# A decoder step on one Trainium2 core: the second MLP product in seven products of half size

## The chip, the cores and the metric

The kernel runs on one core of a Trainium2 chip. Its engines are TensorE (PE, matmuls; its weight loads are shown as PEld), VectorE (DVE), ScalarE (ACT), GpSimd (POOL) and SyncE (SP), whose queue issues most of the DMAs. Matmuls write to PSUM; everything else lies in SBUF or in DRAM. The metric is the device time of one execution in microseconds, the median of the runs shown.

## What is computed

One step of a decoder trunk with 1024 prompt tokens and 8 samples, all in fp32, T = 1032 columns in all. The change is in the last part, a gated MLP with a residual, followed by a norm:

```python
h = rmsnorm(x, g_ffn) * (1.0 + sc_f) + sh_f
a, b = jnp.split(h @ w_ffn_in, [D_FF], axis=-1)        # D_FF = 2816
...  # acc: causal convolution of width 3 over a
f = (jax.nn.silu(acc + conv_b) * b) @ w_ffn_out        # 2816 -> 1024
x = x + gt_f * f
...
yp = rmsnorm(yp, g_final); ys = rmsnorm(ys, g_final)
```

## The kernel before

Activations lie with channels on the 128 partitions and tokens in columns. A token half is HALF = 516 columns, a quarter QUART = 258; NS = 8 sample columns end the second half. An fp32 operand is split into two fp32r tiles, high and low: `split2` (L824) makes the high one with a cast on ScalarE and the low one with a subtraction on VectorE. A product is then three matmuls: high by high, high by low, low by high.

The first MLP product (L949 to L951 in `prod`, tiles pA and pS) already runs as seven products of half size (Winograd's form of Strassen's scheme). Its moving operands B11, B21, B22 and T1 to T4 are sums of quarters of h, made once; its weights A11, A12, A22 and S1 to S4 are quarters of a weight tile or sums of them, which GpSimd forms (L1099). The work goes f tile by f tile (FT = 22 tiles of 128 channels), seven steps of 24 matmuls each. `go` (L1254) does a step: it loads weights ten steps ahead, issues the products, splits one later weight (`prep`), and evacuates the result from PSUM (`evac`). After step A12 and S4 the convolution follows (L1149, L1154 and L1157), and `out_f` (L1159) multiplies the two branches on GpSimd and stores a half of an f tile to the DRAM tile `fd`, laid out by f.

The second product (L1402 to L1422) reads f and the weights back in groups of 2 to 4 f tiles (FFN_GROUPS). For each group it goes over 4 quarters and 8 output tiles m: `ffn_mm` does 3 matmuls per f tile, and `add_gated` (L1337) adds the result, times the gate, to a tile of xs, which `load_x` (L1316) loads from `x2d`. So each group adds to all of xs anew. In the last group the final norm follows quarter by quarter (`last_steps`, `final_a` to `final_last`).

PSUM serves both products through `banks` (L918), a ring of four tiles of two banks each. SBUF pools: `m0p` has four slots, which B11 and B21 hold until the last f tile; `gr` (12 slots) takes the place of the pools of the first product; `rw` has four buffers for what has just been loaded. `load2` and `split_f` load and split a tile; the first group's are put four steps before the end of the first product. The instructions of each engine are ordered by a scheduler, which goes by the order of the program and by when operands are ready.

## Time and profile before

| | |
|---|---|
| median of 3 runs | 1283.18 us (1282.71 to 1284.1) |
| profiled execution | 1283.75 us, its span 1282.0 us |
| TensorE busy | 1236.0 us in 9640 matmuls |
| VectorE, ScalarE, GpSimd busy | 821.0, 450.8, 389.8 us |
| mean granted clock of TensorE | 0.982 of full speed |

The span is the time from the first to the last instruction; the other 1.75 us of the profiled execution lie around it. A line such as L1379 is a line of the kernel. A row of a group gives the line, engine, operation, output and inputs, shapes and count, then busy time and the mean of one, and then the idle time of the engine just before it with what ended it.

### The profile page before, as it was taken

What the parts mean: (1) busy time and instruction counts of PE and PEld (TensorE: products, weight loads), DVE (VectorE), ACT (ScalarE), POOL (GpSimd) and SP (SyncE); (2) the same over time, 40 slices, a digit from 0 to 9 for tenths busy, and PEclk for the clock granted to TensorE, in tenths of its full rate; (3) what the DMA queues carried; (4) which work ended last, traced back from release to release, by engine and by line L of the source; (5) the groups of instructions that cost most, each with busy time, mean ns of one, the idle gap of its engine ahead of it and who ended that gap; (6) DMA issues with size and microseconds to landing.
All of it is one profiled execution on the core that took longest, in us unless ns stands there. A gap on an engine that the chain in (4) does not pass through costs nothing.

```text
span 1282.0 us, 24007 instructions
## 1 busy us (share of the span) xinstructions
PE 1236.0 (96%) x9640; PEld 1199.7 (94%) x9640; DVE 821.0 (64%) x1647; ACT 450.8 (35%) x878; POOL 389.8 (30%) x381
## 2 busy tenths in 40 slices
PE   8899999999999999968999999999999799999996
PEld 6799999999999999868999999999999799999996
DVE  4875556465753522789778777777777766676345
ACT  4453343342423411454334333343434301122053
POOL 3441111111330011464645545454553000000033
PEclk9999999999999999889999999999999899999998
DMA  8725444444410543102412222131224623332002
GB/s 319 273 59 178 122 137 156 125 140 152 143 44 1 207 151 106 39 28 74 145 64 99 75 76 78 71 100 63 88 75 141 238 83 100 100 128 71 1 34 100
DMA packets 78079, 140.57 MB, mean 110 GB/s; under 512 B 10928, under 2 KB 50064, under 8 KB 77968
## 3 DMA queue, kind: packets, MB, share of 16 engines
q1 hardware_dynamic: 74624, 138.09, 32.7%
q8 instruction: 76, 1.25, 0.4%
q10 hardware_dynamic: 3344, 0.95, 0.3%
q14 instruction: 35, 0.29, 0.1%
HBM read 115.00 MB, written 24.01 MB: 108 GB/s over the span
## 4 chain that ended last, share of the span: by engine, by line
PE 85%; DVE 7%; POOL 3%; DMA 2%; issue 1%; ACT 1%; DVEq 0%; SPq 0%; POOLq 0%; ACTq 0%
PE z L333 7%; PE z L334 7%; PE z L335 7%; PE fo L1379 6%; PE pS L949 6%; PE pS L951 6%; PE pS L950 6%; PE fo L1381 6%; PE fo L1380 6%; PE pA L950 5%; PE pA L949 5%; PE pA L951 5%; PE mo L949 2%; PE mo L951 2%; PE mo L950 2%; PE ada_ps L237 1%
## 5 line engine op out<-in xcount | busy, mean ns | idle before, releaser
L1379 PE MATMUL fo<-fhl,whl 128*128 128x258 f32 x704 | 198.0, 290 | 9.4 <-DVE xs L1344 9.1
L333 PE MATMUL z<-h_hi,hi_in 128*128 128x384 f32 (+1 forms) x624 | 203.7, 329 | 0.6 <-ACT h_hi L361 0.6
L334 PE MATMUL z<-h_lo,hi_in 128*128 128x384 f32 (+1 forms) x624 | 199.6, 320 | 0.2 <-DVE h_lo L362 0.2
L335 PE MATMUL z<-h_hi,lo_in 128*128 128x384 f32 (+1 forms) x624 | 198.7, 319 | 0.1
L1380 PE MATMUL fo<-fhl,whl 128*128 128x258 f32 x704 | 197.4, 283 | 0.0
L1381 PE MATMUL fo<-fhl,whl 128*128 128x258 f32 x704 | 195.4, 283 | 0.0
L949 PE MATMUL pS<-T,w_S 128*128 128x258 f32 x528 | 150.8, 286 | 6.5 <-ACT T L825 4.7
L950 PE MATMUL pS<-T,w_S 128*128 128x258 f32 x528 | 150.4, 285 | 5.0 <-DVE T L822 5.0
L951 PE MATMUL pS<-T,w_S 128*128 128x258 f32 x528 | 150.1, 284 | 0.0
L1344 DVE SCALAR_TENSOR_TENSOR xs<-fo,modT,xs 128x258 f32<-128x258 f32 (+1 forms) x224 | 104.5, 480 | 68.3 <-PE fo L1381 66.1
L1379 PEld LDWEIGHTS fo<-fhl,whl 128*128 128x128 f32 x704 | 132.3, 190 | 12.3 <-DVE xs L1344 10.3
L1380 PEld LDWEIGHTS fo<-fhl,whl 128*128 128x128 f32 x704 | 134.1, 190 | 0.0
L1381 PEld LDWEIGHTS fo<-fhl,whl 128*128 128x128 f32 x704 | 132.6, 190 | 0.0
L333 PEld LDWEIGHTS z<-h_hi,hi_in 128*128 128x128 f32 x624 | 117.2, 188 | 14.8 <-issue 12.8
L1161 POOL TENSOR_TENSOR mix_all<-mix_all 128x516 f32<-128x516 f32 x44 | 63.2, 1438 | 184.6 <-DVE mix_all L1115 159.6
L334 PEld LDWEIGHTS z<-h_lo,hi_in 128*128 128x128 f32 x624 | 117.9, 189 | 1.4 <-DVE h_lo L362 1.0
L335 PEld LDWEIGHTS z<-h_hi,lo_in 128*128 128x128 f32 x624 | 117.4, 188 | 0.5 <-DVE lo_in L215 0.4
L949 PEld LDWEIGHTS pS<-T,w_S 128*128 128x128 f32 x528 | 101.1, 191 | 7.3 <-ACT T L825 4.9
L950 PEld LDWEIGHTS pS<-T,w_S 128*128 128x128 f32 x528 | 101.0, 191 | 5.5 <-DVE T L822 5.5
L825 ACT CAST w_S<-S 128x512 fp32r<-128x512 f32 x88 | 54.5, 620 | 142.3 <-PE pS L951 87.9
L951 PEld LDWEIGHTS pS<-T,w_S 128*128 128x128 f32 x528 | 101.2, 192 | 0.0
L1154 DVE SCALAR_TENSOR_TENSOR mix_all<-mix_all,pa 128x508 f32<-128x508 f32 (+1 forms) x80 | 91.2, 1140 | 7.1 <-ACT mix_all L1149 4.9
(249 smaller groups left out, 3129.8 us busy)
## 6 DMA issues: line engine op xcount, KB each, us to landing
raw_ada<-w_ada SPq DMA_DIRECT2D x64, 256.0 KB, 3.5
raw_in<-w_in SPq DMA_DIRECT2D x26, 512.0 KB, 4.2
raw_a<-w_fin SPq DMA_DIRECT2D x25, 512.0 KB, 3.6
fd<-mix_all SPq DMA_DIRECT2D x44, 258.0 KB, 2.9
raw_fo<-fd SPq DMA_DIRECT2D x22, 516.0 KB, 4.5
raw_b<-w_fin SPq DMA_DIRECT2D x22, 512.0 KB, 3.6
raw_wo<-w_fout SPq DMA_DIRECT2D x22, 512.0 KB, 4.3
x2d<-mix_all SPq DMA_DIRECT2D x16, 258.0 KB, 2.4
```

Source lines behind the costliest of these rows:

```text
L333: mm(ps[:, 0:n], hi[:, ws], xh[:, k, 0:n], start=first, stop=False)
L334: mm(ps[:, 0:n], hi[:, ws], xl[:, k, 0:n], start=False, stop=False)
L335: mm(ps[:, 0:n], lo[:, ws], xh[:, k, 0:n], start=False, stop=last)
L949: mm(o, w[0][:, ks], b[:, 0, cols], start=first and kk == 0, stop=False)
L950: mm(o, w[0][:, ks], b[:, 1, cols], start=False, stop=False)
L951: mm(o, w[1][:, ks], b[:, 0, cols], start=False, stop=end)
L1154: nc.vector.scalar_tensor_tensor(s[:, 0:np_], a[:, i:i + np_], cw(i, f), s[:, 0:np_], ALU.mult, ALU.add)
L1161: nc.gpsimd.tensor_tensor(s, s, Bt.pop((f, t)), op=ALU.mult)
L1344: nc.vector.scalar_tensor_tensor(dst[:, 0:np_], ps[:, 0:np_], gt_f[:, m, 0:1], dst[:, 0:np_], ALU.mult, ALU.add)
L1379: mm(o, w[:, 0, ms_], v[:, 0, cols], start=i == 0, stop=False)
L1380: mm(o, w[:, 0, ms_], v[:, 1, cols], start=False, stop=False)
L1381: mm(o, w[:, 1, ms_], v[:, 0, cols], start=False, stop=i == len(fs) - 1)
```

## The change

The second product takes the same form as the first. Its output (1024 channels by 1032 columns) is cut in two by channels (4 m tiles each) and by columns (HALF each), and its inner dimension in two by f tiles: tile k with tile k + 11, for FH = 11 values of k. Seven products follow in the order of OUT_PRODS. In each, k is the outer loop, and four PSUM tiles collect all 4 m by 2 quarters; the last NLATE = 3 values of k run m by m, so that tiles end one after another.

The moving operands B11, B21, B22 and T1 to T4 of this product are made where f is made. The f tiles now come in pairs (FSEQ: 0, 11, 1, 12, ...). After an f tile `out_f` stores three of the four quarters, and the differences T1 to T4 are made on VectorE (`sum_t`), one per step of `go`, from the queue `late`; each is stored to `fd`, which now holds 7 x 11 tiles of half width. The weight sums S1 to S4 are made as the weights come in (`split_o`): S1 and S4 on GpSimd, S2 and S3 on VectorE. Operands come in 77 pairs (moving tile and weight), loaded and split NAHEAD = 8 pairs ahead (`ahead`). The first four go into m0p, and are split four steps before the end of the first product.

Results are kept as running sums in SBUF (Uo and W5) and added to xs, which is loaded from x2d in four parts of 4 m tiles by half. The final norm runs over halves and quarters in the last product. The diff, cut to its core:

```diff
+FH = FT // 2
+OUT_PRODS = (("A11", "B11"), ("A12", "B21"), ("S1", "T1"), ("S2", "T2"), ("S4", "B22"), ("S3", "T3"), ("A22", "T4"))
+FSEQ = tuple(f for k in range(FH) for f in (k, k + FH))
+
+NLATE = 3
+NAHEAD = 8
...
-    fd = dp.tile([FT, P, T], F32, tag="fd", name="fd")
+    fd = dp.tile([len(OUT_PRODS) * FH, P, HALF], F32, tag="fd", name="fd")
+    FD = {b: i * FH for i, (_, b) in enumerate(OUT_PRODS)}
...
     def out_f(f, t):
         s = Ft.pop((f, t))
         nc.gpsimd.tensor_tensor(s, s, Bt.pop((f, t)), op=ALU.mult)
-        nc.sync.dma_start(fd[f, :, t * HALF:(t + 1) * HALF], s)
+        k, i = f % FH, f // FH
+        Fo[k, i, t] = s
+        if (i, t) != (0, 1):
+            store_f(("B11", "B21", "B22")[i + t], k, s)
+        if (k, i, 1 - t) in Fo:
+            late.extend([lambda: sum_t(k, "T1", (0, 0), (0, 1), (0, 0))] if i == 0 else [
+                lambda: sum_t(k, "T3", (0, 1), (1, 1), (0, 1)), lambda: sum_t(k, "T2", (1, 1), (1, 1), (0, 0)),
+                lambda: sum_t(k, "T4", (1, 0), (1, 0), (1, 1))])
+
+    def store_f(name, k, s):
+        nc.sync.dma_start(fd[FD[name] + k], s)
+
+
+    Fo, late = {}, deque()
+
+    def sum_t(k, name, dst, a, b):
+        for i, t in {a, b}:
+            assert vown[vidx[f"f{k + FH * i}_{t}"]] == f"f{k + FH * i}_{t}"
+        nc.vector.tensor_tensor(Fo[k, dst[0], dst[1]], Fo[k, a[0], a[1]], Fo[k, b[0], b[1]], op=ALU.subtract)
+        store_f(name, k, Fo[k, dst[0], dst[1]])
...
-    HELD = (0, 1)
+    HELD = FSEQ[0:2]
     order = [(f, n) for n in ("S4", "S2", "S3", "S1", "A22") for f in HELD]
-    order += [(f, n) for f in range(2, NLEAD) for n in NAMES[2:]]
-    order += [(f, n) for f in range(NLEAD, FT) for n in NAMES]
+    order += [(f, n) for f in FSEQ[2:NLEAD] for n in NAMES[2:]]
+    order += [(f, n) for f in FSEQ[NLEAD:] for n in NAMES]
...
     def go(n, ev=True):
@@ -1259,12 +1288,14 @@
         prep()
         if ev:
             evac(f, name)
+        if late:
+            late.popleft()()
...
+    items = [(p, k) for p in range(len(OUT_PRODS)) for k in range(FH)]
+    WSRC = {"A11": (0, 0), "A12": (1, 0), "S1": (1, 1), "S2": (0, 0), "S4": (1, 0), "S3": (1, 1), "A22": (1, 1)}
...
+    def load_o(n=1):
+        for _ in range(min(n, len(to_load))):
+            p, k = to_load.popleft()
+            wn, bn = OUT_PRODS[p]
+            i, j = WSRC[wn]
+            v = oraw[p, k] = rw.tile([P, T], F32, tag="raw", name=f"raw_o{p}_{k}")
+            nc.sync.dma_start(v[:, 0:HALF], fd[FD[bn] + k])
+            if wn == "S1":
+                nc.sync.dma_start(sb[:, k], w_fout[k, :, 512:1024])
+            nc.sync.dma_start(v[:, HALF:HALF + 512], w_fout[k + FH * i, :, j * 512:(j + 1) * 512])
+
+    def split_o(n=1):
+        for _ in range(min(n, len(to_split))):
+            p, k = to_split.popleft()
+            wn = OUT_PRODS[p][0]
+            v = oraw.pop((p, k))
+            w = v[:, HALF:HALF + 512]
+            if wn == "S1":
+                nc.gpsimd.tensor_tensor(sb[:, k], sb[:, k], w, op=ALU.add)
+                w = sb[:, k]
+            elif wn == "S2":
+                nc.vector.tensor_tensor(sb[:, k], sb[:, k], w, op=ALU.subtract)
+                w = sb[:, k]
+            elif wn[0] == "S":
+                (nc.gpsimd if wn == "S4" else nc.vector).tensor_tensor(w, w, sb[:, k], op=ALU.subtract)
+            if k < 4:
+                u = m0p.tile([P, 2, 2, HALF], F32R, tag="m", name=f"o{p}_{k}")
+            else:
+                u = gr.tile([P, 2, 2, HALF], F32R, tag="g", name=f"o{p}_{k}")
+            ou[p, k] = u[:, 0], u[:, 1, :, 0:512]
+            split2(ou[p, k][0], v[:, 0:HALF])
+            split2(ou[p, k][1], w)
...
     for n in range(8, len(order)):
         go(n)
         if n == len(order) - 4:
+            load_o(4)
+            split_o(4)
+    while late:
+        late.popleft()()
...
+    gr = ctx.enter_context(tc.tile_pool(name="gr", bufs=8, side="right", reuse_waits="tile"))
+    uo = ctx.enter_context(tc.tile_pool(name="uo", bufs=1, side="right", reuse_waits="tile"))
+    f2 = ctx.enter_context(tc.tile_pool(name="f2", bufs=3, reuse_waits="tile"))
...
+    sb = uo.tile([P, FH, 512], F32, name="sb")
+    W5 = uo.tile([P, 4, HALF], F32, name="w5")
+    acc3 = [uo.tile([P, HALF], F32, name=f"acc3_{t}") for t in range(2)]
+    R3 = [uo.tile([P, HALF], F32, name=f"R3_{t}") for t in range(2)]
+    Uo = e1p.tile([P, 4, HALF], F32, tag="e", name="uo")
+    xs = vxp.tile([P, KT, 1036], F32, tag="v", name="xs")
...
+    def out_mm(o, p, k, m, s, first, last):
+        b, w = ou[p, k]
+        cols = slice(s * QUART, (s + 1) * QUART)
+        ms_ = slice(m * P, (m + 1) * P)
+        mm(o, w[:, 0, ms_], b[:, 0, cols], start=first, stop=False)
+        mm(o, w[:, 0, ms_], b[:, 1, cols], start=False, stop=False)
+        mm(o, w[:, 1, ms_], b[:, 0, cols], start=False, stop=last)
...
+    def before(name):
+        if name == "A12":
+            for m in range(4):
+                gated(m, 0, Uo[:, m])
+        elif name == "S4":
+            st12 = uo.tile([P, 4, NS], F32, name="st12")
+            nc.vector.tensor_tensor(st12, Uo[:, :, SC], W5[:, :, SC], op=ALU.add)
+            for m in range(4):
+                gated(m, 1, Uo[:, m, 0:HALF - NS])
+                gated(m, 1, W5[:, m, 0:HALF - NS])
+            return st12
+        elif name == "S3":
+            for m in range(4):
+                gated(m + 4, 1, W5[:, m, 0:HALF - NS])
+        elif name == "A22":
+            for m in range(4):
+                gated(m + 4, 0, Uo[:, m])
+
+    def after(name, m, ps, st):
+        v = ps[:, :, 0:QUART]
+        if name == "A11":
+            nc.scalar.copy(two(Uo[:, m]), v)
+        elif name == "A12":
+            gated(m, 0, v)
+            sq_sum(m, 0, m == 0, nc.gpsimd)
+        elif name == "S1":
+            nc.scalar.copy(two(W5[:, m]), v)
+        elif name == "S2":
+            nc.vector.tensor_tensor(two(Uo[:, m]), v, two(Uo[:, m]), op=ALU.add)
+        elif name == "S4":
+            gated(m, 1, v)
+            nc.vector.tensor_tensor(st[:, m], ps[:, 1, QUART - NS:QUART], st[:, m], op=ALU.add)
+            if m == 3:
+                gated_samples(0, st)
+                for i in range(4):
+                    sq_sum(i, 1, i == 0, nc.gpsimd)
+        elif name == "S3":
+            nc.vector.tensor_tensor(two(Uo[:, m]), v, two(Uo[:, m]), op=ALU.add)
+            gated(m + 4, 1, Uo[:, m, 0:HALF - NS])
...
+    def ahead(i):
+        load_o(max(0, i + NAHEAD + 3 - (len(items) - len(to_load))))
+        split_o(max(0, i + NAHEAD + 1 - (len(items) - len(to_split))))
+
+    XLOADS = {(0, 7): (0, 0), (2, 0): (0, 1), (3, 0): (4, 1), (4, 0): (4, 0)}
+    for p, (wn, bn) in enumerate(OUT_PRODS[:-1]):
+        ps = [banks(f"o{p}_{m}") for m in range(4)]
+        st = None
+        for k in range(FH - NLATE):
+            ahead(p * FH + k)
+            for m in range(4):
+                for s in range(2):
+                    out_mm(ps[m][:, s, 0:QUART], p, k, m, s, k == 0, False)
+            if (p, k) in XLOADS:
+                m, t = XLOADS[p, k]
+                nc.sync.dma_start(xs[:, m:m + 4, t * HALF:(t + 1) * HALF], x2d[:, m:m + 4, t * HALF:(t + 1) * HALF])
+            if k == 5:
+                st = before(wn)
+        for m in range(4):
+            ahead(p * FH + FH - NLATE + m)
+            for s in range(2):
+                for k in range(FH - NLATE, FH):
+                    out_mm(ps[m][:, s, 0:QUART], p, k, m, s, False, k == FH - 1)
+            after(wn, m, ps[m], st)
...
+    for s in range(2):
+        pair = [banks(f"o{p}_{s}_{i}") for i in range(2)]
+        n = FH - (5 if s else NLATE)
+        for k in range(n):
+            if s == 0:
+                ahead(p * FH + k)
+            last_k(s, k, pair)
...
+            if s == 0 and k == 7:
+                fin_R(1, 2, 0)
+                for m in range(KT):
+                    fin_m(m, 1, 0, HALF, nc.gpsimd)
...
+        for m in range(4):
+            for k in range(n, FH):
+                last_k(s, k, pair, m, m + 1)
+            last_m(s, m, pair)
```

## Rows read from the trace of the kernel before

**Rows 1.** Busy time, share and count by engine, page.

```profile
PE 1236.0 (96%) x9640; PEld 1199.7 (94%) x9640; DVE 821.0 (64%) x1647; ACT 450.8 (35%) x878; POOL 389.8 (30%) x381
```

**Rows 2.** The chain that ended last, by engine, page.

```profile
PE 85%; DVE 7%; POOL 3%; DMA 2%; issue 1%; ACT 1%; DVEq 0%; SPq 0%; POOLq 0%; ACTq 0%
```

**Rows 3.** Groups of instructions: matmuls of the second product (busy us, mean ns).

```profile
L1379 PE MATMUL fo<-fhl,whl 128*128 128x258 f32 x704 | 198.0, 290 | 9.4 <-DVE xs L1344 9.1
L1381 PE MATMUL fo<-fhl,whl 128*128 128x258 f32 x704 | 195.4, 283 | 0.0
```

**Rows 4.** Windows (length; PE, PEld, DVE, ACT, POOL; granted clock, DMA share, GB/s).

```profile
700.00:800.00 100.00, 100.00 (x836) 100.00 (x835) 75.38 (x105) 37.75 (x60) 51.68 (x50) 1.00 0.24 80
...
1020.00:1165.00 145.00, 144.87 (x1199) 144.34 (x1198) 94.24 (x232) 25.21 (x25) 0.00 (x0) 1.00 0.31 99
```

**Rows 5.** Timeline of PE in the second product (start, length, instruction, wait before).

```profile
995.00 0.28 PE L1379 MATMUL fo<-fhl,whl 128*128 128x258 f32 x1
...
1011.52 0.58 PE L1379 MATMUL fo<-fhl,whl 128*128 128x258 f32 x1 [6.28 <-DVE xs L1344]
...
1268.31 0.39 PE L1379 MATMUL fo<-fhl,whl 128*128 128x258 f32 x1 [1.01 <-DVE xs L1344]
...
1269.74 0.28 PE L1381 MATMUL fo<-fhl,whl 128*128 128x258 f32 x1
```

**Rows 6.** Waits of PE from 600 us on (total us, times, longest).

```profile
PE fo L1379 <- DVE xs L1344: 9.1, 4, 6.3
```

**Rows 7.** Timeline of DVE at the start of the second product.

```profile
1010.98 1.67 DVE L1344 SCALAR_TENSOR_TENSOR xs<-fo,modT,xs 128x258 f32<-128x258 f32 x4 [1.83 <-DMA xs<-x2d]
```

**Rows 8.** Windows after the long wait and around the 1.01 us wait.

```profile
1011.50:1017.00 5.50, 5.47 (x26) 5.48 (x27) 2.61 (x6) 0.00 (x0) 0.00 (x0) 0.53 1.07 364
...
1265.00:1270.00 5.00, 3.99 (x31) 3.60 (x29) 3.94 (x11) 2.74 (x7) 4.21 (x6) 1.00 0.32 107
```

**Rows 9.** Timeline of ACT: casts of operands around the second product's start.

```profile
992.36 1.06 ACT L825 CAST fhl<-raw_fo 128x1032 fp32r<-128x1032 f32 x1 [4.99 <-PE pA L951]
...
996.66 1.03 ACT L825 CAST whl<-raw_wo 128x1024 fp32r<-128x1024 f32 x1
...
1018.62 1.06 ACT L825 CAST fhl<-raw_fo 128x1032 fp32r<-128x1032 f32 x1 [10.72 <-DMA raw_fo<-fd]
```

**Rows 10.** Timeline of DVE: two half-width splits, one behind the other.

```profile
582.42 0.68 DVE L822 SCALAR_TENSOR_TENSOR w_S<-S,w_S 128x512 fp32r<-128x512 f32 x1
583.02 0.69 DVE L822 SCALAR_TENSOR_TENSOR T<-mix_all,T 128x516 fp32r<-128x516 f32 x1
```

**Rows 11.** DMA issues: count, KB each, us to landing.

```profile
raw_fo<-fd SPq DMA_DIRECT2D x22, 516.0 KB, 4.5
```

**Rows 12.** Groups of VectorE instructions, shapes apart.

```profile
L1344 DVE SCALAR_TENSOR_TENSOR xs<-fo,modT,xs 128x258 f32<-128x258 f32 x168 | 78.3, 483 | 68.3 <-PE fo L1381 66.1 <-DMA xs<-x2d 1.8
...
L215 DVE TENSOR_TENSOR lo_in<-raw_in,hi_in 128x1024 fp32r<-128x1024 f32 x25 | 30.9, 1235 | 6.4 <-ACT hi_in L214 5.3 <-PE rc L675 1.0
...
L822 DVE SCALAR_TENSOR_TENSOR whl<-raw_wo,whl 128x1024 fp32r<-128x1024 f32 x22 | 27.3, 1241 | 1.4 <-ACT whl L825 1.4
```

**Rows 13.** Timeline of POOL at the end of an f tile.

```profile
736.53 1.79 POOL L1099 TENSOR_TENSOR S<-S,raw_a 128x512 f32<-128x512 f32 x1
739.15 1.30 POOL L1161 TENSOR_TENSOR mix_all<-mix_all 128x516 f32<-128x516 f32 x1 [0.83 <-ACT mix_all L1157]
```

**Rows 14.** Timeline of DVE in the same stretch.

```profile
736.29 0.21 DVE L1156 SCALAR_TENSOR_TENSOR mix_all<-scv,pa,mix_all 128x8 f32<-128x8 f32 x1
...
737.09 1.25 DVE L1156 SCALAR_TENSOR_TENSOR mix_all<-scv,pa,mix_all 128x8 f32<-128x8 f32 x1
...
739.59 0.70 DVE L1115 TENSOR_TENSOR mix_all<-pA,mix_all 128x516 f32<-128x516 f32 x1 [0.64 <-ACT mix_all L1119]
740.20 0.81 DVE L822 SCALAR_TENSOR_TENSOR w_S<-S,w_S 128x512 fp32r<-128x512 f32 x1
```

**Rows 15.** Window of 20 us early in the first product.

```profile
580.00:600.00 20.00, 17.06 (x135) 16.15 (x133) 20.00 (x29) 9.13 (x15) 7.87 (x9) 1.00 0.27 79
```

More of the change, by code (lines that the diff above doesn't have):

```diff
@@ L1265, in trunk_step @@
         if k == 0:
[L1266 to L1267 removed]
+            for i, f in enumerate(HELD):
+                go(i)
                 PS0[f] = PS.pop(f)
@@ L1293, in trunk_step @@
         ev_c12a(f)
-    for f in range(NLEAD):
+    for f in FSEQ[:NLEAD]:
         fin_c11(f)
@@ new lines, in gated @@
+    def gated(m, t, v, a=0, b=None):
+        b = (HALF - NS if t else HALF) if b is None else b
+        d = xv(m, t, a, b)
+        if len(v.shape) == 3:
+            if b - a == HALF:
+                d = two(d)
+            else:
+                nc.vector.scalar_tensor_tensor(d[:, 0:QUART], v[:, 0, 0:QUART], gt_f[:, m, 0:1], d[:, 0:QUART], ALU.mult, ALU.add)
+                v, d = v[:, 1, 0:b - QUART], d[:, QUART:b]
+        nc.vector.scalar_tensor_tensor(d, v, gt_f[:, m, 0:1], d, ALU.mult, ALU.add)
@@ new lines, in gated_samples, with sq_sum @@
+    def gated_samples(m0, st):
+        nc.vector.tensor_tensor(st, st, gt_f[:, m0:m0 + 4, 1:NCOND], op=ALU.mult)
+        d = xs[:, m0:m0 + 4, T - NS:T]
+        nc.vector.tensor_tensor(d, d, st, op=ALU.add)
+    def sq_sum(m, t, first, eng, a=0, b=HALF):
+        v = xv(m, t, a, b)
+        acc = acc3[t][:, a:b]
+        if first:
+            nc.scalar.activation(acc, v, AF.Square)
+        else:
+            s = small(f"sq3_{m}_{t}_{a}")[:, a:b]
+            nc.scalar.activation(s, v, AF.Square)
+            eng.tensor_tensor(acc, acc, s, op=ALU.add)
+        nc.scalar.activation(v, v, AF.Copy, scale=pa[:, PA_GFIN + m:PA_GFIN + m + 1])
@@ new lines, in after @@
+    def after(name, m, ps, st):
[19 more added lines that the diff above has]
+            gated(m + 4, 1, Uo[:, m, 0:HALF - NS])
+            if m == 3:
+                st = uo.tile([P, 4, NS], F32, name="st22")
+                nc.vector.tensor_tensor(st, Uo[:, :, SC], W5[:, :, SC], op=ALU.add)
+                gated_samples(4, st)
+                for i in range(4):
+                    sq_sum(i + 4, 1, False, nc.vector)
```

173 lines of the change are left out of this document (54 added, 119 removed).

## The prediction

> **What bounds the kernel now.** I read the busy line of the page first, then the chain of waits, then windows of the two stretches that the change touches. TensorE is busy for 1236.0 of 1282.0 us and VectorE for 821.0 [rows 1]; the chain that ended last is 85% TensorE [rows 2]. The reader should see in them that matmuls one after another set the end, and that something else does so only in a few places. The change takes matmuls out of the second MLP product (called stage 2 here) and puts VectorE work and transfers into the first (stage 1). So two questions remain: what a matmul is worth in stage 2, and whether the other engines keep up in both.
>
> What a matmul is worth is not its mean duration of 283 to 290 ns [rows 3], because matmuls overlap. From 1020 to 1165 us there are 1199 in 145.00 us with TensorE busy for 144.87 [rows 4]: one every 0.1209 us. In stage 1 there are 836 in 100 us [rows 4], 0.1196 us each.
>
> Stage 2 begins at 995.00 and its last matmul starts at 1269.74 [rows 5], 275 us for 2112 matmuls, which at 0.1209 need 255.3. Part of the rest is four waits of TensorE for the add of a result to xs, 9.1 us together [rows 6], of which one lasts 6.28 and another 1.01 [rows 5]. The long one ends when VectorE gets a tile of xs from a DMA [rows 7]: the adds need x2d, whose load is late. In the 5.5 us after it the mean granted clock is 0.53, so nearly all of it at the 1.2 GHz level, and there are 26 matmuls [rows 8], which take 3.1 us at 0.1209: 5.47 - 3.1 = 2.3 us lost. Around the 1.01 us wait the clock stays at 1.00, or 2.4 GHz [rows 8].
>
> **The change, part by part.** *Matmuls.* Before: 22 f tiles, 8 m, 4 quarters, 3 each = 2112. After: 7 products, 11 k, 4 m, 2 s, 3 each = 1848. All have 258 columns, as before, so 264 go, at 0.1209 us: -31.9 us. A bank now gets 3 matmuls in a row before the next one, where fo had 6 to 12 and the products of stage 1 had 12; no row shows three of this width. Since 1199 in 145 us and 836 in 100 us differ by 1% for 9 and for 12 in a row, I take no cost, and for the bounds 1% either way, 2 us.
>
> *The four waits.* The first product, A11, is copied by ScalarE to SBUF and needs no x2d; x2d comes in four loads of 4 m tiles by half, each well ahead of its first use. So 9.1 us of waits and 2.3 us of slow clock go, if nothing new is late at the start. What is next late there: four operand pairs lie in m0p slots, which the last f releases after its A11 and A12 matmuls, before stage 2. They last 4 x 24 x 0.1209 = 11.6 us. The fifth needs a gr slot; the row nearest to it is ScalarE's first cast into that pool at 992.36, and the next at 996.66 [rows 9]. From 996.7 one pair costs VectorE 2 x 0.6 us (two splits start 0.60 us apart [rows 10]), so the fifth is ready near 999 and is wanted at 1006.6. A raw load could be late instead; with the 4.5 us that one takes to land [rows 11] the pair is still in time. I take -11.4, with 0 as the other end.
>
> *Operands in stage 2.* 77 pairs replace 44 tiles: 154 half splits of about 0.6 us, 94 us of VectorE, for 44 of about 1.24 [rows 12], 55 us. Per pair TensorE takes 24 x 0.1209 = 2.90 us; VectorE needs 1.2 us, and 1.8 with a weight sum (S2, S3; 22 sums). The 224 adds of 0.48 us [rows 12] and 112 small ones become about 60 of half width. So VectorE's sum falls, and eight pairs ready ahead (23 us) cover uneven stretches. GpSimd's 22 weight sums (S1, S4) are like its operations of 1.3 to 1.8 us in stage 1 [rows 13], against 2.90.
>
> *Transfers.* 77 x 514 KB + 11 x 256 KB is 43 MB over some 224 us, 195 GB/s, and 270 in S1, the worst product. The trace moves 364 GB/s where several loads queue [rows 8], and a load lands in 4.5 us [rows 11]; a raw buffer has 4 x 2.9 = 11.6 us. SP's queue holds these loads behind the x2d loads; a 1 MB load of those costs some 3 us of flow, which the eight pairs cover. I take 0; uncovered, each of the four would cost up to those 3 us, 12 in all.
>
> *Handing over PSUM.* A product fills all four tiles of `banks`, so the next one starts only as they are read. The last three k run m by m: 18 matmuls, 2.2 us per m. Tile 3 is wanted 18 matmuls, 2.2 us, after its last matmul. In that stretch VectorE has, per m, the splits (1.2) and the result (0.6): 1.8 us, it keeps up. Behind S4 a weight sum and a second add make it 3 us; at A12 and S2 a sum on GpSimd runs beside it. The trace shows what that does: GpSimd's sum starts at 736.53 for 1.79 us [rows 13], and an 8-column operation of VectorE beside it lasts 1.25 us, where the same operation took 0.21 just before [rows 14]. So at three boundaries VectorE needs up to 4 us per m against 2.2, and tile 3 is read about 2 us late; at the other three it isn't. +6 us, bounds 0 and 26 (three waits like the 6.28 us one with its 2.3).
>
> The Trainium skill, "SBUF — State Buffer", section "SBUF: two separate sides", says of the port that VectorE and GpSimd share that one operation holds it whole and the other blocks. The 1.25 us row agrees; by that rule every sum moved to GpSimd still takes its time from VectorE: 22 x 1.5 = 33 us in stage 2.
>
> *Stage 1.* 44 differences on VectorE and 33 more stores of 258 KB (8.7 MB at a DMA share of 0.24 [rows 4]: no cost, and at most a few us if they delayed weight loads, which are issued ten steps, 28 us, ahead). No row has such a difference of 516 columns; the nearest is the one of 1024 with both operands in SBUF, 1.24 us [rows 12], so 0.62. An f lasts 7 x 24 x 0.1196 = 20.1 us, of which VectorE is idle for 24.6% [rows 4], 4.9 us. Two differences take 1.24. A wait comes with them: the first difference after an f needs GpSimd's product, which starts at 739.15 and lasts 1.30 [rows 13], so it can begin at 740.5, while VectorE ended its convolution at 738.3 [rows 14]. If VectorE stands there it is 2.2 us, and behind it in VectorE's queue are the next weight split and the add that empties PSUM, for which TensorE waits. But 1.24 + 2.2 = 3.4 is less than 4.9, and four PSUM tiles let the adds be late by 3 steps, 8.6 us. 0 in the steady stretch. The first pair is different: VectorE has no idle time from 580 to 600 us and TensorE is busy for only 17.06 [rows 15]; four differences there are 2.5 us, half hidden by then: +1.2, bounds 0 and 5.
>
> *The end.* The last quarter goes through the same steps (square, sum, power, scale, store): 0. GpSimd has eight products of 516 columns queued ahead of a power that TensorE waits for; eight at 1.3 us end about when it is wanted: 0, at most 3.
>
> Sum: -31.9 - 11.4 + 6 + 1.2 = -36.1, a span of 1245.9 us. The profiled execution took 1283.75 for its span of 1282.0, and is 0.57 above the median of 1283.18: span + 1.2 = 1247.1. I say 1247.
>
> **Rivals.** (a) *The start of stage 2 stays late*: the fifth pair, held by a pool slot or a load, takes the place of x2d. For it: ScalarE waited 10.7 us for a raw load at 1018.62 [rows 9]. Against: that load was queued behind 3 MB of x2d, which moves. The 11.4 us stay: 1258.
>
> (b) *The boundaries cool the clock*: the three heavy ones wait as long as the 6.28 us row and pay 2.3 after it: 3 x 8.6 in place of 6: 1267. Against: the 1.01 us wait left the clock at 1.00. The Trainium skill, "TensorE: Matmul & The Clock Gate", section "A second HAM failure mode: psum-queue depth-cycling", reports a kernel in which short idle times between groups as PSUM tiles rotate made the clock go up and down. The 1.01 us row speaks against that here.
>
> (c) *VectorE becomes the bound of stage 1* (the one that ends slower): it stands at two waits per f and meets GpSimd's sums at both differences: 1.24 + 2 x 2.2 + 1.8 = 7.4 us against 4.9 idle, 2.5 per f, times 22: 55 us, 1302. It decides from 4.9 us per f on, and the kernel is slower than before from 4.9 + 36/22 = 6.5. Against: at 739.59 an add goes ahead of a split whose operand is late [rows 14], so the order is made by readiness, and a difference whose operand is late needn't stand in front.
>
> (d) *Everything is hidden*: no boundary waits, 1241. That the change keeps all its matmuls is excluded by the loops.
>
> **How the numbers follow.** Forecast 0.56 (1243 to 1253), (a) 0.14, (b) 0.12, (c) 0.10 (0.04 of it slower, most of the rest between 1262 and 1280), (d) 0.08. About 0.2%, 2.6 us, is what a measurement can tell from no change. Slower 0.04, same 0.02, faster 0.94. The range goes from (d) to just beyond (b): 1238 to 1268.
>
> **What would show it.** 1848 matmuls at 0.121 us; no wait over 1 us and a granted clock of 1.00 in the first 20 us of stage 2; waits of about 2 us behind A12, S2 and S4 only; VectorE near 82% in stage 1 with TensorE still at 836 per 100 us. A rate there of under 830 means (c). Most likely to be wrong is the cost of the boundaries, as it rests on the order in which VectorE gets its work.

## The result, and the profile after

The median went from 1283.64 us (1282.71 to 1284.12; the three runs of the table above and one more) to 1242.97 us (1241.46 to 1243.39); the ratio is 0.9682, with a 95% interval of 0.9665 to 0.9699. That is 40.7 us less. The profiled execution of the kernel after took 1241.46 us for a span of 1239.7; it is the shortest of its four, 1.5 us under the median.

First the page: TensorE's busy line, and the group of the first of the three matmuls.

```profile
PE 1199.9 (97%) x9376; PEld 1164.9 (94%) x9376; DVE 845.0 (68%) x1537; ACT 487.3 (39%) x971; POOL 424.4 (34%) x395
...
L1394 PE MATMUL o<-o 128*128 128x258 f32 x616 | 175.5, 285 | 3.4 <-DVE xs L1408 1.9
```

9640 matmuls became 9376, 264 fewer. TensorE is busy for 36.1 us less than in [rows 1], VectorE for 24 more. In the group, where [rows 3] had 9.4 us of idle time, 3.4 are left.

Windows of the kernel after (length; PE, PEld, DVE, ACT, POOL; granted clock, DMA share, GB/s), the first two in stage 1, the others in stage 2:

```profile
580.00:600.00 20.00, 16.97 (x124) 16.22 (x122) 20.00 (x29) 9.13 (x15) 7.88 (x9) 0.91 0.24 79
700.00:800.00 100.00, 100.00 (x836) 100.00 (x835) 80.91 (x113) 36.82 (x60) 50.98 (x50) 1.00 0.29 96
1000.00:1020.00 20.00, 20.00 (x169) 20.00 (x168) 15.17 (x24) 11.11 (x19) 1.96 (x1) 1.00 0.98 318
1020.00:1060.00 40.00, 38.86 (x322) 38.43 (x321) 32.15 (x40) 21.52 (x38) 18.07 (x11) 1.00 0.95 319
1060.00:1100.00 40.00, 38.86 (x324) 38.65 (x324) 29.39 (x44) 21.25 (x38) 7.36 (x6) 1.00 0.73 239
1100.00:1150.00 50.00, 49.84 (x415) 49.64 (x415) 42.43 (x58) 21.14 (x38) 13.47 (x9) 1.00 0.58 180
1120.00:1130.00 10.00, 9.84 (x83) 9.64 (x82) 9.89 (x16) 3.33 (x6) 0.02 (x1) 1.00 0.18 57
1150.00:1200.00 50.00, 49.79 (x416) 49.62 (x415) 35.07 (x65) 24.00 (x43) 4.12 (x4) 1.00 0.41 127
```

Stage 1 runs at 836 matmuls per 100 us, as in [rows 4], with VectorE at 81% in place of 75%. Stage 2 holds a clock of 1.00 throughout, and from 1100 us on there are 415 matmuls in 50 us, 0.1205 us each. Its first 60 us have the DMA engines busy for 95 to 98%.

PE's timeline in stage 2 (start, length, instruction, wait before): the first matmul, the first of S1 (1060.67), all waits of 0.4 us or more, and the last matmul.

```profile
995.68 0.28 PE L1394 MATMUL o<-o 128*128 128x258 f32 x1
...
1029.55 0.39 PE L1394 MATMUL o<-o 128*128 128x258 f32 x1 [0.62 <-ACT uo L1447]
1031.08 0.39 PE L1394 MATMUL o<-o 128*128 128x258 f32 x1 [0.53 <-ACT uo L1447]
1060.67 0.28 PE L1394 MATMUL o<-o 128*128 128x258 f32 x1
1064.13 0.39 PE L1394 MATMUL o<-o 128*128 128x258 f32 x1 [1.14 <-DVE xs L1408]
1224.99 0.39 PE L1394 MATMUL o<-o 128*128 128x258 f32 x1 [0.80 <-DVE xs L1408]
...
1226.76 0.28 PE L1396 MATMUL o<-o 128*128 128x258 f32 x1
```

So stage 2 takes 231.1 us where [rows 5] give 274.7: 43.7 less. It starts 0.7 us later than before, and what comes behind it takes 12.9 us in place of 12.3. The waits stand at the start of A12 (0.62 + 0.53, for ScalarE's copies of A11's results) and at the start of S1 (1.14, for VectorE's adds of A12's results). At the start of S4 there is 0.2 us and behind S4 none. The wait of 0.80 is that of 1.01 in [rows 5], in the last quarter.

What the readers of PSUM did just before these two waits, ScalarE first, then VectorE, and GpSimd beside it:

```profile
1026.80 0.62 ACT L831 CAST o<-raw_o 128x516 fp32r<-128x516 f32 x1 [2.48 <-DMA raw_o<-fd]
1027.63 1.37 ACT L831 CAST o<-raw_o 128x512 fp32r<-128x512 f32 x2 [0.21 <-DMA raw_o<-w_fout]
1028.91 0.58 ACT L1447 COPY uo<-o 128x516 f32<-128x516 f32 x1
```

```profile
1061.95 1.46 DVE L828 SCALAR_TENSOR_TENSOR o<-raw_o,o 128x516 fp32r<-128x516 f32 x1 [1.21 <-ACT o L831]
1063.33 0.74 DVE L1408 SCALAR_TENSOR_TENSOR xs<-o,modT,xs 128x516 f32<-128x516 f32 x1
```

```profile
1061.55 1.31 POOL L1423 TENSOR_TENSOR acc<-acc,sq 128x516 f32<-128x516 f32 x1 [0.23 <-ACT sq L1422]
```

At A12 the copy that frees a PSUM tile stands behind three casts, and the first of these stood 2.48 us at a load. At S1 the add of the last tile stands behind a split that waited 1.21 us for its cast and then took 1.46 us, twice what splits take elsewhere (0.69). What GpSimd does beside this split is not a weight sum, the last of which ended at 1057.9, but the sum of squares of A12's results for the final norm (L1423); the split ends 0.55 us after it.

### The profile page after: what moved, and what is told of

Read it like the earlier page. It is cut to its first block, busy times and chain, and to the rows that moved or that the text cites. A ratio compares the mean times of both kernels' runs of the same rounds, so it can differ in the third digit from the quotient of the medians.

```text
span 1239.7 us, 23791 instructions
## 1 busy us (share of the span) xinstructions
PE 1199.9 (97%) x9376; PEld 1164.9 (94%) x9376; DVE 845.0 (68%) x1537; ACT 487.3 (39%) x971; POOL 424.4 (34%) x395
## 3 DMA queue, kind: packets, MB, share of 16 engines
q1 hardware_dynamic: 93632, 167.07, 40.7%
q8 instruction: 74, 1.21, 0.4%
## 4 chain that ended last, share of the span: by engine, by line
PE 80%; DVE 9%; DMA 4%; POOL 3%; issue 2%; ACT 1%; SPq 0%; DVEq 0%; POOLq 0%; ACTq 0%
PE z L339 8%; PE z L340 7%; PE z L341 7%; PE pS L955 6%; PE pS L957 6%; PE pS L956 6%; PE pA L956 5%; PE pA L955 5%; PE pA L957 5%; PE o L1394 3%; PE o L1396 3%; PE o L1395 3%; DMA raw_o<-w_fout 2%; PE mo L955 2%; PE mo L956 2%
## 5 line engine op out<-in xcount | busy, mean ns | idle before, releaser
L1394 PE MATMUL o<-o 128*128 128x258 f32 x616 | 175.5, 285 | 3.4 <-DVE xs L1408 1.9
L1395 PE MATMUL o<-o 128*128 128x258 f32 x616 | 173.9, 282 | 0.0
L1396 PE MATMUL o<-o 128*128 128x258 f32 x616 | 173.8, 282 | 0.0
L1394 PEld LDWEIGHTS o<-o 128*128 128x128 f32 x616 | 116.4, 189 | 4.7 <-DVE xs L1408 2.7
L1395 PEld LDWEIGHTS o<-o 128*128 128x128 f32 x616 | 116.8, 190 | 0.0
L1396 PEld LDWEIGHTS o<-o 128*128 128x128 f32 x616 | 116.6, 189 | 0.0
L828 DVE SCALAR_TENSOR_TENSOR o<-raw_o,o 128x516 fp32r<-128x516 f32 (+1 forms) x132 | 97.6, 775 | 21.8 <-ACT o L831 21.4
L831 ACT CAST o<-raw_o 128x516 fp32r<-128x516 f32 (+1 forms) x132 | 76.8, 621 | 83.1 <-PE o L1396 36.4
```

Source lines behind the costliest of these rows:

```text
L828: nc.vector.scalar_tensor_tensor(dst, a, 1.0, b, ALU.mult, ALU.subtract)
L831: nc.scalar.copy(dst[:, 0], src)
L1394: mm(o, w[:, 0, ms_], b[:, 0, cols], start=first, stop=False)
L1395: mm(o, w[:, 0, ms_], b[:, 1, cols], start=False, stop=False)
L1396: mm(o, w[:, 1, ms_], b[:, 0, cols], start=False, stop=last)
```

## The experiments

Two more sets of runs of the kernel after gave medians of 1244.54 us (ratio 0.9693, 0.9675 to 0.9711), where 1243 within 1 us had been expected, and, from the kernel of experiment 9, 1242.77 (0.9683, 0.967 to 0.9696). So differences of under 2 us between variants of it are not told apart by the medians here; waits in a trace are.

### 1. What the waits for x2d were worth

The kernel before with the residual left out: the first group writes to xs in place of adding.

```diff
-            load_x(0, e1p.tile([P, KT, QUART], F32, tag="e", name="xs0"))
+            xs[0] = e1p.tile([P, KT, QUART], F32, tag="e", name="xs0")
...
-                    add_gated(q, m, ps[:, s])
+                    add_gated(q, m, ps[:, s], g == 0)
```

> The kernel before, in which the first group of the second product writes its gated result to xs and doesn't add it to x2d, which isn't loaded (the residual is left out of y). Theory (the prediction's term of the four waits): the 9.1 us of waits for xs and the 2.3 us of slow clock go, nothing else is late in their place: 11.4 us less, about 1272 us, and no wait over 1 us in the first 30 us of the second product. Rival: the loads and splits of the second group are late too and take the place of x2d; then 3 to 6 us less, about 1279, with a wait of TensorE for a split.

1273.96 us, 0.9926 (0.9913 to 0.9938): -9.5 us. Its waits of PE for xs, and the window over the start of stage 2:

```profile
PE fo L1384 <- DVE xs L1349: 1.0, 1, 1.0
PE fo L1384 <- DVE xs L1343: 0.9, 2, 0.7
...
990.00:1020.00 30.00, 28.99 (x236) 28.27 (x235) 24.94 (x51) 11.57 (x12) 2.72 (x4) 1.00 0.48 149
```

The long wait and the slow clock behind it are gone, and 1.9 of the 9.1 us stay for other reasons (1.0 is the wait in the last quarter). 9.1 + 2.3 - 1.9 = 9.5, what was measured (the interval is 8.0 to 11.2).

### 2. What 264 matmuls are worth

The kernel before without the third matmul for m = 0, 1, 2 (22 x 3 x 4 = 264; the low part of the weight is left out there).

```diff
-            mm(o, w[:, 1, ms_], v[:, 0, cols], start=False, stop=i == len(fs) - 1)
+            if m >= 3:
+                mm(o, w[:, 1, ms_], v[:, 0, cols], start=False, stop=i == len(fs) - 1)
```

> The kernel before without the third matmul (low weight by high operand) of output tiles 0 to 2 in the second product: 264 matmuls of 258 columns fewer, as many as the change takes away; everything else is as it was (part of the product is left out). Theory: a matmul is worth 0.120 to 0.121 us there: 31.7 to 31.9 us less, about 1252. Rival: VectorE's adds (0.48 us and more for every 0.72 us of matmuls in the thinned groups) set the pace of part of the product: 20 us less or fewer, 1263 and over.

1253.16 us, 0.9768 (0.9753 to 0.9783): -30.4 us. The same view of waits as in [rows 6]:

```profile
PE fo L1379 <- DVE xs L1344: 10.0, 4, 7.3
PE fo L1379 <- DVE gs_f L1342: 1.1, 2, 0.7
```

The waits for xs grew by 0.9 us, and 1.1 us of waits for the gated samples are new, so the matmuls gave 32.4, or 0.123 us each; the interval is 1.9 us wide to either side, so this agrees with the 31.9 of the sum. Experiments 1 and 2 together are 39.9 of the 40.7 us, within some 2.5 us by their intervals: what the change adds costs about what else it saves.

### 3. What stage 1's additions cost

The kernel before with f tiles in pairs, 44 differences on VectorE and 44 more stores (33 in the change).

```diff
+        nc.vector.tensor_tensor(Fo[k, dst[0], dst[1]], Fo[k, a[0], a[1]], Fo[k, b[0], b[1]], op=ALU.subtract)
+        nc.sync.dma_start(fx[n * FH + k], Fo[k, dst[0], dst[1]])
```

> The kernel before with stage 1's part of the change alone: f tiles in the order of pairs, the 44 differences on VectorE, one per step, and 44 more stores of 258 KB to a DRAM tile that nothing reads; the second product is as before. Theory: all of it lies in VectorE's idle time of 4.9 us per f, but for the first pair: 0 to 1.2 us more, 1283.6 to 1285, VectorE near 81% of 700 to 900 us, TensorE still at 836 matmuls per 100 us. Rival (c): VectorE stands at GpSimd's product and meets its sums: 20 to 55 us more, fewer than 830 per 100 us.

1286.37 us, 1.002 (1.0012 to 1.0029): +2.9 us. A window in stage 1 and the wait for xs:

```profile
700.00:800.00 100.00, 100.00 (x836) 100.00 (x835) 81.34 (x113) 36.82 (x60) 50.99 (x51) 1.00 0.30 104
...
PE fo L1400 <- DVE xs L1365: 11.6, 4, 8.9
```

The rate is that of [rows 4]. The wait for x2d grew by 2.5 us, from 9.1 to 11.6, and that wait isn't in the changed kernel. So some 0.4 us are left for stage 1 itself, which the interval of the 2.9 us (1.5 to 3.7) doesn't tell from nothing, and rival (c) falls.

### 4. The kernel after without the 44 subtractions

T1 to T4 are stored unsubtracted.

```diff
-        nc.vector.tensor_tensor(Fo[k, dst[0], dst[1]], Fo[k, a[0], a[1]], Fo[k, b[0], b[1]], op=ALU.subtract)
```

> The changed kernel without the 44 differences on VectorE: the quarters are stored in their place (so y is not the reference's); stores, loads and matmuls are the same. Theory: the differences lie in VectorE's idle time but for the first pair: 0 to 1 us less, 1242 to 1243. Rival: VectorE's waits for GpSimd's product delay the operands of the end of stage 1 and the start of stage 2: 3 us less or more.

1242.57 us, 0.9688 (0.9673 to 0.9703), like the kernel after. VectorE has 75.50 us in 700:800 in place of 80.91, and TensorE 836 matmuls either way: the subtractions lie in idle time. One wait is longer than in the kernel after, that at S1's start, for VectorE's adds:

```profile
1064.22 0.39 PE L1393 MATMUL o<-o 128*128 128x258 f32 x1 [2.81 <-DVE xs L1407]
...
1061.45 0.69 DVE L1355 TENSOR_TENSOR sb<-sb,raw_o 128x512 f32<-128x512 f32 x1 [2.89 <-DMA raw_o<-w_fout]
```

Here the adds stand behind two weight differences of S2 that wait for loads, 2.89 and 0.66 us; GpSimd stretches none of these operations.

### 5. PSUM tiles that end close together

```diff
-NLATE = 3
+NLATE = 1
```

> The changed kernel with NLATE = 1 in place of 3: in the first six products the four PSUM tiles end 0.72 us after one another in place of 2.2, so VectorE and ScalarE must read a tile in 0.72 us. Theory R (the reads go ahead of splits that aren't ready, and a read is 0.6 to 0.7 us): waits of TensorE of at most 1 us at a boundary, 2 where a product needs two operations per tile (A12, S4): 1243 to 1247 us. Theory P (as predicted: between two reads VectorE does the splits of a pair, 1.2 us and more): tile 3 is read 3 us late or more at each of six boundaries, 1258 us and over, and the granted clock falls there.

1247.96 us, 0.9733 (0.972 to 0.9746): 3.4 us over the set of the kernel after that ran beside it, just above what the theory that the reads keep up allowed, and far under the other's 1258. Most of it stands at one place, the start of A12:

```profile
1029.31 0.42 PE L1394 MATMUL o<-o 128*128 128x258 f32 x1 [3.10 <-ACT uo L1447]
1029.30:1033.00 3.70, 3.69 (x18) 3.69 (x19) 3.70 (x7) 3.70 (x8) 0.10 (x1) 0.54 0.96 304
1020.00:1040.00 20.00, 16.90 (x128) 16.69 (x127) 16.18 (x21) 11.64 (x22) 5.63 (x4) 0.91 0.91 305
```

The wait is 3.10 us, and the matmuls behind it start 0.21 us apart in place of 0.12, which is the 1.2 GHz level. 20 us held 128 matmuls, where the kernel after had 155 there. By the starts of the products, A12 takes 3.1 us longer than in the set beside it and S1 1.0 less, and the last product, which NLATE shapes too, 1.5 longer. At S1, S2 and S4 no wait is over 0.3 us, although the tiles end 6 matmuls apart in place of 18: VectorE's speed at the boundaries has room, and A12's start has another cause.

### 6. Loading four pairs ahead

```diff
-NAHEAD = 8
+NAHEAD = 4
```

> The changed kernel with four operand pairs ready ahead in place of eight. Theory: building up eight pairs is what fills the DMA (share 0.95 to 0.98 from 1000 to 1060 us) and lets ScalarE stand at a load before it copies the tiles of A11; with four the burst is shorter, the two waits of TensorE there (1.15 us) go, and four pairs (11.6 us) still cover: 1240 to 1243 us. Rival: eight are needed, because a sum on GpSimd, three loads per pair in S1 and the loads of x2d make stretches longer than 11.6 us in which pairs come late: waits of TensorE for splits, 1248 us and over.

1242.38 us, 0.9679 (0.9666 to 0.9692): no difference. The DMA share stays at 0.99 in 1000:1020 and 0.97 in 1040:1060, and the waits at 1.7 us (ScalarE's copies) and 2.2 us (VectorE's adds). Neither theory's signs came. The edit hardly changed what runs: in the traces, 9 of SyncE's 542 transfers, 6 of ScalarE's 980 instructions and 21 of VectorE's 1537 have another place in the order. So the constant doesn't set how far ahead the loads run, and the buffers were the next candidate.

### 7. More transfers, first attempt

256 KB of weight copied from DRAM to DRAM for each pair from A12 on.

```diff
+            if p:
+                nc.sync.dma_start(junk[FH * p + k], w_fout[k + FH * i, :, j * 512:(j + 1) * 512])
```

> The changed kernel with one more transfer for each f of products A12 to S3: 256 KB of the second product's weight are copied once more, from DRAM to DRAM, on the queue of the raw loads (66 copies, 17.3 MB that nothing reads). Between 1100 and 1150 us the changed kernel moved 180 GB/s at a DMA share of 0.58, between 1020 and 1060 us 319 GB/s at 0.95, and one f of a product takes TensorE 24 x 0.12 = 2.9 us; the copy adds 256 KB to each. My theory: the 0.95 of the start is loading ahead and not need, so the flow has room: 180 + 0.262 MB / 2.9 us (90 GB/s) = 270 GB/s is under the 319 that was seen, the pairs still come in time, and the time is 1243 to 1248 us, with a DMA share over 0.8 to 1200 us. Rival: stage 2 is close to the limit of its transfers; then TensorE waits for the splits and casts behind late loads at every f of the products after A12, 0.3 us or more each, and the time is over 1263 us.

1249.01 us, 0.9734 (0.9721 to 0.9747). The time is in the range of the theory, but it says nothing on it. From 100 to 200 us the DMA share of this kernel is 0.73 (229 GB/s), where the kernel after has 0.48 (151). The copies depend on nothing and ran in the first 200 us. Stage 2 began at 1001.10, 5.4 us later than in the kernel after, which is nearly all of the 6 us. From 1100 to 1150 us its DMA share was 0.57, without the copies 0.58.

### 8. The weight sums of S1 and S4 on VectorE

```diff
-                nc.gpsimd.tensor_tensor(sb[:, k], sb[:, k], w, op=ALU.add)
+                nc.vector.tensor_tensor(sb[:, k], sb[:, k], w, op=ALU.add)
...
-                (nc.gpsimd if wn == "S4" else nc.vector).tensor_tensor(w, w, sb[:, k], op=ALU.subtract)
+                nc.vector.tensor_tensor(w, w, sb[:, k], op=ALU.subtract)
```

> The changed kernel with the sums and differences of the weight's halves for S1 and S4 (22 instructions, 1.65 and 1.51 us each) on VectorE instead of GpSimd. My theory: they hide at either engine. VectorE is busy for a third of stage 2 and would take 22 x about 0.6 = 13 us more; the time is that of the changed kernel, 1241 to 1246 us, and the wait before S1 stays at about 1.1 us. Rival: GpSimd's sums hold the VectorE up while both work on SBUF, and the splits of the changed kernel take 0.75 to 0.81 us against a pitch of 0.60 in the kernel before for that reason: then the splits' mean in products S1 and S4 falls by 0.15 us or more and the time by 1 to 3 us. Second rival: VectorE's copies at the boundaries come later for the added work: waits of 1 us or more at S1 and S4 and 2 to 5 us more.

1242.05 us, 0.968 (0.9667 to 0.9693): the time of the kernel after. But the rows moved. Splits from 1030 to 1060 us (busy, mean ns) and the window of stage 2, first of the kernel after, then of this one; its last row is the window behind the wait at A12:

```profile
L828 DVE SCALAR_TENSOR_TENSOR o<-raw_o,o 128x516 fp32r<-128x516 f32 (+1 forms) x14 | 12.6, 921 | 0.0
L828 DVE SCALAR_TENSOR_TENSOR o<-sb,o 128x512 fp32r<-128x512 f32 x9 | 10.8, 1196 | 2.0 <-ACT o L831 1.8
...
995.00:1227.00 232.00, 228.44 (x1892) 226.72 (x1890) 166.70 (x250) 110.75 (x196) 64.91 (x50) 1.00 0.64 209
```

```profile
L828 DVE SCALAR_TENSOR_TENSOR o<-raw_o,o 128x516 fp32r<-128x516 f32 (+1 forms) x15 | 10.1, 693 | 2.2 <-ACT o L831 1.4 <-DMA raw_o<-w_fout 0.7
L828 DVE SCALAR_TENSOR_TENSOR o<-sb,o 128x512 fp32r<-128x512 f32 x9 | 6.1, 686 | 0.1
...
995.00:1227.00 232.00, 229.43 (x1891) 228.09 (x1890) 166.09 (x272) 110.58 (x196) 30.58 (x28) 0.99 0.65 209
...
1032.00:1036.00 4.00, 4.00 (x23) 4.00 (x23) 3.92 (x7) 2.06 (x4) 0.00 (x0) 0.60 0.89 262
```

Without GpSimd's sums beside them the splits take 690 ns in place of 921 and 1196. VectorE does 22 operations more and is busy for no longer (166.1 against 166.7 us; that is 72% of stage 2, not a third). The theory that the sums hide was right for the time, the rival (they hold VectorE up) right for the splits.

The wait at the start of S1 is gone, but not for want of the sums. TensorE, VectorE and GpSimd there:

```profile
1062.50 0.28 PE L1394 MATMUL o<-o 128*128 128x258 f32 x1
...
1062.64 1.35 DVE L828 SCALAR_TENSOR_TENSOR o<-raw_o,o 128x516 fp32r<-128x516 f32 x1 [1.33 <-ACT o L831]
1063.91 0.74 DVE L1408 SCALAR_TENSOR_TENSOR xs<-o,modT,xs 128x516 f32<-128x516 f32 x1
...
1062.12 1.32 POOL L1423 TENSOR_TENSOR acc<-acc,sq 128x516 f32<-128x516 f32 x1 [0.47 <-ACT sq L1422]
```

As in the kernel after, the add stands behind a split that waits for its cast and runs beside the sum of squares. The add starts 0.58 us later than there, but TensorE begins S1 1.83 us later (1062.50 against 1060.67), so it no longer has to wait. It is late from A12: waits of 0.93 and 0.54 us there were followed by four microseconds at a clock of 0.60, with 23 matmuls where the kernel after has 36.

### 9. The reads of PSUM given priority

```diff
-            after(wn, m, ps[m], st)
+            with tc.high_priority():
+                after(wn, m, ps[m], st)
```

> The changed kernel, but the instructions that take a finished PSUM bank out (those after each output block) go ahead of the casts and splits of later pairs in the order in which each engine gets its work. My theory: the waits of 1.15 us before A12 and 1.14 us before S1 are there because the copy or add that frees the first bank stands behind casts or splits, one of which waits for a load. With the reads first both waits fall under 0.4 us, the waits of TensorE on ScalarE for uo are gone, and the time falls by about 2 us, to 1240 to 1242.5. Rival: the order isn't the cause, the banks are read at the speed that the first matmuls of the next product fill them (about 2 us on any engine): the waits stay at 1 us or more and the time at 1243 to 1245. Second rival: the reads stand at the head of the queue and hold the splits up that the next product's first matmuls need: the wait moves to the operands and the time is 1244 to 1250.

1242.77 us, 0.9683 (0.967 to 0.9696). The edit moved no instruction on any engine, so the question stays unanswered by it and the run is a repeat of the kernel after. As such it shows how far the waits differ from one execution to the next: 1.65 + 0.54 us at A12 and 1.62 at S1, where the first had 1.15 and 1.14. The granted clock stayed at 1.00 behind them.

### 10. Nine operand buffers in place of twelve

```diff
-    gr = ctx.enter_context(tc.tile_pool(name="gr", bufs=8, side="right", reuse_waits="tile"))
+    gr = ctx.enter_context(tc.tile_pool(name="gr", bufs=5, side="right", reuse_waits="tile"))
```

> The changed kernel with 5 buffers instead of 8 in the pool of stage 2's operands (9 instead of 12 with the four taken over from stage 1). My theory, after loading four instead of eight pairs ahead changed neither the burst of transfers nor the waits: the number of free buffers sets how far the loads run ahead. With 9 the stretch of a DMA share over 0.9 ends before 1050 us, where it lasted to 1075 us, the casts that stand at a load by A12 and S1 become fewer, and the time is 1241 to 1244.5. Rival: the buffers are needed: with fewer, the operands come just in time, TensorE waits for casts and splits at many f's, and the time is over 1248 us.

1254.37 us, 0.9776 (0.9756 to 0.9797), 11 us over the kernel after: the rival's time, but not by its mechanism. Waits for casts and splits sum to 1.8 us; what is new stands at boundaries. PE behind S2 and behind S4, ScalarE before A12, VectorE behind S2, and a window:

```profile
1127.33 0.39 PE L1394 MATMUL o<-o 128*128 128x258 f32 x1 [2.20 <-DVE uo L1454]
1130.08 0.58 PE L1394 MATMUL o<-o 128*128 128x258 f32 x1 [1.49 <-DVE uo L1454]
...
1166.06 0.36 PE L1394 MATMUL o<-o 128*128 128x258 f32 x1 [1.34 <-DVE st L1457]
1170.54 0.36 PE L1394 MATMUL o<-o 128*128 128x258 f32 x1 [0.89 <-DVE st L1457]
...
1023.93 1.08 ACT L1447 COPY uo<-o 128x516 f32<-128x516 f32 x2
1025.57 3.24 ACT L831 CAST o<-raw_o 128x516 fp32r<-128x516 f32 x6 [0.55 <-PE o L1396]
...
1125.03 1.63 DVE L1408 SCALAR_TENSOR_TENSOR xs<-w,modT,xs 128x508 f32<-128x508 f32 x1
...
1120.00:1130.00 10.00, 6.39 (x49) 5.89 (x47) 8.03 (x9) 3.85 (x7) 7.40 (x5) 0.89 0.46 137
1130.00:1140.00 10.00, 9.44 (x59) 9.26 (x60) 9.51 (x15) 1.03 (x2) 1.29 (x1) 0.77 0.50 160
```

The share from 1020 to 1060 us fell from 0.95 to 0.86, as the theory wanted, but it is 0.97 to 0.99 from 1050 to 1070. Two things follow. At A12 the scheduler put the copies of the first three tiles ahead of the casts, and the wait there is gone: the order of copies and casts makes it. At S2 GpSimd's sums for S4 now run beside the boundary (POOL 7.40 us of 10, against 0.02 in the kernel after), VectorE's operations stretch from 0.74 to 1.06 and 1.63 us, the split in front of the first add waits 1.83 us for a cast that itself waits 1.90 us for one of these sums, and TensorE waits 4.2 us (2.20, 1.49 and 0.48). In the 10 us behind the first two waits the clock is at 0.77. Behind S4 TensorE waits 2.2 us (1.34 and 0.89); GpSimd does nothing there. In front of the adds stand a weight difference on VectorE that waited 1.74 us for a load, and six splits.

### 11. More transfers, second attempt

The high half of each pair's weight operand is written to DRAM (256 KB, 66 times), so the transfer can't start before its cast.

```diff
+            if p:
+                nc.scalar.dma_start(junk[FH * p + k], ou[p, k][1][:, 0].bitcast(F32))
```

> The changed kernel with one more transfer for each f of products A12 to A22: the rounded half of the weight operand (256 KB, 66 times, 17.3 MB) is written from SBUF to DRAM, where nothing reads it, by ScalarE's queue. The copies from DRAM to DRAM tried before depended on nothing and ran in the first 200 us of the kernel; this one can't start before its operand is cast, so it falls into stage 2. One f of a product takes TensorE 24 x 0.12 = 2.9 us, so the writes add some 90 GB/s to the 180 GB/s of 1100 to 1150 us. My theory: the DMA share of 0.95 at the start of stage 2 is loading ahead and not need. With the writes the pairs are loaded less far ahead, but 270 GB/s is under the 318 GB/s that was seen there, so they still come in time: a DMA share over 0.8 in 1100:1150 and a time of 1243 to 1249 us. Rival: stage 2 is close to the limit of its transfers: TensorE waits for splits and casts that stand at late loads, 0.3 us or more at most f's of S1 to A22, and the time is over 1258 us.

1262.29 us, 0.9835 (0.9821 to 0.9848), 19 us over the kernel after. Windows, the longest wait of PE, and ScalarE's cast before it:

```profile
1020.00:1060.00 40.00, 34.44 (x263) 33.93 (x262) 24.77 (x32) 18.45 (x32) 10.39 (x8) 0.91 1.00 344
1060.00:1100.00 40.00, 34.75 (x256) 33.77 (x255) 23.52 (x34) 19.04 (x32) 9.73 (x7) 0.87 0.97 332
1100.00:1150.00 50.00, 48.20 (x398) 47.60 (x397) 40.85 (x53) 20.22 (x36) 18.37 (x11) 1.00 0.76 244
...
1032.84 0.46 PE L1397 MATMUL o<-o 128*128 128x258 f32 x1 [5.04 <-ACT uo L1450]
...
1029.94 0.62 ACT L831 CAST o<-raw_o 128x516 fp32r<-128x516 f32 x1 [4.10 <-DMA raw_o<-fd]
```

My theory falls for A12 and S1, and the rival's time came without its sign: only one wait of TensorE, 0.55 us, is for a cast, and the others stand at boundaries. From 1020 to 1100 us there are 519 matmuls where the kernel after has 646: 127 x 0.12 = 15 us of the 19. From 1100 to 1200 us 802 stand against 831, 3.5 us, at a share of 0.76 to 0.84: there the transfers have room. The wait at A12 grew from 1.15 to 5.6 us (5.04 + 0.52), again behind a cast that stood at a load, 4.10 us in place of 2.48; the waits at S1 grew from 1.14 to 5.3. But the edit does more than move bytes. Each write takes ScalarE 0.33 us to issue, and one stands between the late cast and the copy, so some 0.4 us of the 5.6 is its. The profile also puts 18.4 us of waits of SyncE's queue, which issues the loads, down to the writes. How much of the 19 us is want of room for transfers, the run doesn't separate.

## Why the prediction was right, and where it wasn't

The forecast was 1247 us, the result 1243. Step by step, from the profiled executions, where the span fell by 42.3 us and the sum had 36.1:

*The price of a matmul* held: three in a row per bank cost nothing (415 in 50 us), and 264 fewer gave 32.4 us by experiment 2 where 31.9 stood.

*The waits for xs* held but for two small ones. No wait over 1 us and a clock of 1.00 in the first 20 us of stage 2, as the prediction asked for; the 0.80 us in the last quarter stays, which the sum had as gone (+0.8). Experiment 1 gives 9.5 for the 11.4. Rival (a) falls: the fifth pair was in time.

*Handing over PSUM* was mis-sized: 2.5 us in place of 6 (-3.5), and 1.15 of the 2.5 stand at a boundary that the sum had at nothing, so the term is nearer than its step, by luck. Behind A12, S2 and S4, where the sum had 2 us each, 1.14, 0.2 and 0 came. What failed is the step that put GpSimd's weight sums beside the reads behind A12 and S2: they were over by 1057.9 and by 1120.0 (POOL 0.02 us in 1120:1130). That GpSimd's work can stretch what stands in front of a read is shown at S1's start, 1.46 us for a split in place of 0.69, but by the sum of squares, and behind 1.21 us in which VectorE stood at a cast. Moving the weight sums away (experiment 8) left both as they were, and in experiment 4 weight differences that wait for loads made 2.81 us at the same place without GpSimd.

Experiment 10 brings the weight sums to S2, where the boundary then costs 4.2 us, twice what the sum had; its 2.2 us behind S4 are VectorE's own work, as the prediction had it there, and a late load. A wait that the prediction left out came at A12's start: ScalarE's copies stand behind casts that wait for loads. Experiment 11 makes it longer by making loads later, experiment 10 takes it away by another order. The prediction had looked at VectorE's queue alone, and named the order of work as the point most likely to be wrong.

*Stage 1* held: 0 in the steady stretch (experiments 3 and 4). Stage 2 starts 0.7 us later where 1.2 stood (-0.5); but the other two profiled executions of the same instructions start it at 994.76 and 994.85, before the 995.00 of [rows 5]. So no run shows the 1.2 us for the first pair, and the 0.7 is this execution's. VectorE was at 81% with 836 matmuls per 100 us.

*Transfers* cost next to nothing, as the sum had it, but for a reason that was weaker than it read. The prediction compared means, 195 GB/s and 270 in S1, with 364. In the first 60 us of stage 2 the flow was 318 GB/s at a share of 0.95 to 0.98, as twelve buffers are filled and x2d and S1's second weight halves come too (with nine buffers the share from 1020 to 1060 us was 0.86). By experiment 11 writes of some 90 GB/s more are not hidden there, though part of its cost is not want of room. The bound of 12 us was the better part of that step.

*The end* cost 0.7 us where 0 stood (bounds up to 3).

*Not in the sum*: stage 2 before took 274.7 us, and 255.3 for matmuls with 11.4 of waits and slow clock leave 8.0. After, 231.1 less 1848 x 0.1209 = 223.4 and less 3.3 of the waits above leave 4.4. So 3.6 us went that no step named (-3.6). The starts of the matmuls show where most of it is. In both kernels some 4.2 us of these remainders go to matmuls of the final norm that stand between the product's own. Most of the rest are matmuls that start about 0.21 us behind the one before them in place of 0.12, outside the waits and the slow clock: 41 before, 11 after, which is 3.9 us against 1.1. 31 of the 41 stand inside an output tile and not at its start, so adds that free PSUM late don't explain them; their cause stays open.

These differences, +0.8 - 3.5 - 0.5 + 0.7 - 3.6 = -6.1, are the 6.2 us by which the span came out shorter than the sum. By the medians it is 4, as the profiled execution is 1.5 us under its own.

Rival (b) did not come: behind 1.1 us waits the clock stayed at 1.00. It was nearer than it looked: in experiments 5, 10 and 11 the clock fell behind waits at boundaries. The Trainium skill, "TensorE: Matmul & The Clock Gate", section "A second HAM failure mode: psum-queue depth-cycling", was set aside on one 1.01 us row; experiment 10 agrees with it, with 0.77 behind boundary waits of 1.5 to 2.2 us. The 1242.97 us lie at the lower edge of the forecast's 1243 to 1253, and nearer to rival (d), 1241, than to 1247. But (d) had no wait at a boundary, and 2.5 us of them came.

## What to carry to other kernels

When a product changes its form, price each boundary between products by what stands in front of the PSUM reads in every reading engine's queue, casts that wait for loads included; what stood there decided between 0 and 4.2 us per boundary here, be it a neighbour's sum (experiment 10) or a late load (experiment 4). Compare a transfer's need with the flow in the stretch where buffers fill, not with the stage's mean. And hold single experiments of parts against the whole: here the matmuls and the waits alone explain 39.9 of 40.7 us, so that all that was added had to cost about what else was saved.
